# Up projections as one wide and one narrow matmul per slice, 1/rms squared on the down results, and engine reads of interleaved operands reordered, in a two-layer decoder trunk

## The chip, the cores and the metric

The kernel runs on one NeuronCore of a Trainium2 chip. The metric is the device time of one execution in microseconds; smaller is better. Before the change three runs gave 563.83, 562.90 and 562.57 us, a median of 562.9 us. One further execution was profiled; the tables and rows below come from it.

## The reference, cut to what matters

The program is a decoder trunk of two layers over 256 tokens of width 1024. Layer 0 mixes tokens with a gated linear recurrence, layer 1 with sparse attention, and each is followed by a squared-ReLU MLP of width 4096. Every sub-layer sees RMS-normalised input.

```
def _rmsnorm(x, g):
    y = xf * lax.rsqrt(jnp.mean(xf * xf, axis=-1, keepdims=True) + RMS_EPS)
    return (y * g.astype(jnp.float32)).astype(x.dtype)
def _sq_relu_mlp(h, w_up, w_down):
    u = jax.nn.relu(h @ w_up)
    return (u * u) @ w_down
for i in range(DEPTH):
    x = x + (_rglru_mixer if i % 2 == 0 else _nsa_mixer)(_rmsnorm(x, norm_mix[i]), ...)
    x = x + _sq_relu_mlp(_rmsnorm(x, norm_ffn[i]), mlp_w_up[i], mlp_w_down[i])
```

The factor 1/rms is one number per token, so it commutes with every matmul over the width; and relu(r z)² = r² relu(z)² for a positive r.

## The kernel before, in words

Activations are kept transposed, 128 channels on the partitions and 256 tokens along the row. The residual is `xt`, eight such chunks. All large products are made in a 32-bit format with a short mantissa (`F32R`), so each operand is held as a high and a low part, and a product is the sum high·high + high·low + low·high.

**Weights.** 181 pieces, mostly 128 x 1024 (512 KB), stream in through one DMA queue into five `raw` buffers. ScalarE casts a piece to `whi`; VectorE subtracts to give `wlo`. Seven buffers each hold them, and splitting runs up to six pieces ahead of use (`LOOK`). One piece feeds one output chunk of an up projection (eight slices of 128 in the inner dimension) or a quarter of a down chunk.

**Products.** `mm3` makes three matmuls of 256 columns per slice into the same half of a PSUM bank: `whi` with the high activations, `whi` with the low ones, `wlo` with the high ones. `mm2` makes two: `whi` with high and low side by side (512 columns, the two halves of a bank), then `wlo` with high (256 columns, added to the second half); the two halves have to be added afterwards. Before the change `mm2` is used in the down projections alone (15 of their 16 output chunks); the up projections, the mixers' projections and the last down chunk of layer 1 use `mm3`.

**Walked operands.** TensorE reads an activation row in the order 0, 128, 1, 129, ... (`walk`), so a token's place in PSUM is interleaved: PSUM place 2a+i holds token 128i+a. An engine that goes from PSUM to a plain row, or from a plain row to something that TensorE has to find in that order, must undo it. Before, the engines read PSUM in its own order (`pairs`) and stepped through the SBUF operands with `walk`, 512 bytes up, then back, at every element. This is so where projections leave PSUM (L679, L740, L796, L911, L923, L960) and where high and low parts are made of activations (L802, L803, `xbh` and `xbl` in `product`, `oh` and `ol` in `pv`).

**Order of the work.** Two sections (recurrence of layer 0; attention of layer 1) are planned: each step is added to a `Plan` with an engine, a cost, keys it reads and writes and a wished-for time; a list scheduler with a seeded shuffle, then six rounds of backward and forward placing, yields one order per engine, which the engines then follow strictly. So a step taken out anywhere can reorder other steps. The MLPs (`mlp`) are written out in order. Each section ends with `lead_in`, the first three up chunks of the MLP behind it, together with the sums of squares for 1/rms (`stats_wide`: two matmuls against ones, a square root on ScalarE with its table loaded beforehand, a reciprocal of 128 x 256 on VectorE).

**An up chunk** ends with `up_post`: VectorE takes relu(z)·(1/rms) out of PSUM into `t` (L796), ScalarE squares it twice, once plain (`u`, L801) and once rounded and walked into the high part (L802), VectorE subtracts for the low part (L803). `tick` puts the next weight split between. **A down chunk** (32 slices) ends with two adds of a PSUM half into `xt` (L538), then the epilogue, which makes the next layer's operands or the output. The last chunk of layer 1 is seeded: two matmuls with the identity (L824, L825) put `xt` into PSUM first, and `finish` takes the final norm from there: squares (L1303), sums by matmuls against ones (L1305 for the other seven chunks, L1306 for this one), square root, reciprocal, and spreading matmuls (L1312, L1314).

## Time and profile before

| Quantity | Value |
|---|---|
| Median of three runs | 562.9 us |
| Profiled execution: time, span | 563.95 us, 561.8 us |
| Mean granted TensorE clock | 0.996 of full |
| TensorE matmul, busy | 550.5 us, 98% of the span, 4422 instructions |
| VectorE, busy | 436.3 us, 78% |
| ScalarE, busy | 358.0 us, 64% |
| DMA, mean | 184 GB/s over the span |

The stages, by the places of their instructions in the trace: recurrence from 0 to about 95 us, up projection of layer 0 to about 175, its down projection to about 259, attention to about 383, up projection of layer 1 to about 467, its down projection to 553.6, then the final norm and the output.

How to read it: the time of the execution includes some 2.15 us outside the span of its instructions. Matmuls overlap one another, so the busy sum of TensorE says little; the distance from one matmul's start to the next one's says what it costs. A row of the timeline has its start, its length, the engine, the line of the code, the operation, output and inputs, shapes, and in brackets the idle time ahead of it with what ended that.

### The profile page before, as it was taken

Reading aid. Unit: us, or ns where it says so; the run is one execution under the profiler, and the core shown is the slowest. Engines: PE = TensorE matmul, PEld = TensorE weight load, DVE = VectorE, ACT = ScalarE, POOL = GpSimd, SP = SyncE. Lnnn points to the kernel's source line nnn. Section 1 sums busy time; section 2 is a strip of 40 time slices with the busy share of each in tenths; the row PEclk is TensorE's granted clock in tenths of the full one; section 3 lists DMA queues with packets and bytes.
Section 4 is the critical chain, followed back from the end, with each engine's and each line's share of the span. In section 5 each row is a group of like instructions: output and inputs, shape, how many; then the busy total and the mean of one; then the engine's idle time right before and its main releaser. Section 6 shows DMA issues by size and latency. Waiting matters only on the chain.

```text
span 561.8 us, 11456 instructions
## 1 busy us (share of the span) xinstructions
PE 550.5 (98%) x4422; PEld 528.5 (94%) x4422; DVE 436.3 (78%) x888; ACT 358.0 (64%) x670; POOL 40.1 (7%) x55
## 2 busy tenths in 40 slices
PE   9999899999999999999999999999999999999995
PEld 9989899999999999999899998989999999999995
DVE  6899999887788476476849999989988887465532
ACT  7699587777666354354646999977776765353321
POOL 1010000000000131131000000000000000142220
PEclk9999999999999999999999999999999999999998
DMA  8927266576566646655675432263586667556402
GB/s 313 409 90 226 83 225 215 174 234 200 191 194 222 223 161 214 225 167 198 219 229 177 143 104 58 76 211 99 200 239 200 191 213 234 182 187 218 158 1 76
DMA packets 33222, 103.61 MB, mean 184 GB/s; under 512 B 3856, under 2 KB 8080, under 8 KB 33168
## 3 DMA queue, kind: packets, MB, share of 16 engines
q1 hardware_dynamic: 32624, 102.42, 55.5%
q8 instruction: 35, 0.57, 0.4%
q10 hardware_dynamic: 544, 0.46, 0.2%
q14 instruction: 19, 0.16, 0.1%
HBM read 99.23 MB, written 1.05 MB: 179 GB/s over the span
## 4 chain that ended last, share of the span: by engine, by line
PE 73%; DVE 18%; DMA 5%; ACT 2%; issue 1%; SPq 0%; POOL 0%; DVEq 0%; ACTq 0%; POOLq 0%
PE bank L333 19%; PE bank L329 13%; PE bank L330 13%; PE bank L328 13%; PE bank L335 9%; DVE wlo L338 4%; DMA raw<-in_dram 3%; DVE pt L1140 2%; DMA gw<-in_dram 2%; DVE pt L1168 2%; DVE xb L683 1%; DMA pt<-tt 1%; DVE tt L911 1%; DVE t L735 1%; PE bank L1036 1%
## 5 line engine op out<-in xcount | busy, mean ns | idle before, releaser
L328 PE MATMUL bank<-hhl,whi 128*128 128x256 f32 x768 | 212.0, 276 | 0.4 <-DVE tt L960 0.4
L330 PE MATMUL bank<-hhl,wlo 128*128 128x256 f32 x768 | 211.5, 275 | 0.0
L329 PE MATMUL bank<-hhl,whi 128*128 128x256 f32 x768 | 211.5, 275 | 0.0
L333 PE MATMUL bank<-uhl,whi 128*128 128x512 f32 x480 | 157.3, 382 | 0.0
L328 PEld LDWEIGHTS bank<-hhl,whi 128*128 128x128 f32 x768 | 147.7, 192 | 0.6 <-DVE tt L960 0.4
L330 PEld LDWEIGHTS bank<-hhl,wlo 128*128 128x128 f32 x768 | 147.7, 192 | 0.0
L329 PEld LDWEIGHTS bank<-hhl,whi 128*128 128x128 f32 x768 | 147.7, 192 | 0.0
L287 DVE TENSOR_TENSOR wlo<-raw,whi 128x1024 fp32r<-128x1024 f32 x115 | 142.8, 1262 | 1.9 <-ACT whi L278 1.9
L335 PE MATMUL bank<-uhl,wlo 128*128 128x256 f32 x480 | 130.8, 273 | 0.0
L278 ACT CAST whi<-raw 128x1024 fp32r<-128x1024 f32 x116 | 120.0, 1056 | 14.1 <-ACT whi L278 11.0
L333 PEld LDWEIGHTS bank<-uhl,whi 128*128 128x128 f32 x480 | 90.7, 189 | 12.6
L335 PEld LDWEIGHTS bank<-uhl,wlo 128*128 128x128 f32 x480 | 92.2, 192 | 0.0
L338 DVE TENSOR_TENSOR wlo<-raw,whi 128x1024 fp32r<-128x1024 f32 (+2 forms) x72 | 77.1, 1091 | 1.9 <-ACT whi L341 1.8
L341 ACT CAST whi<-raw 128x1024 fp32r<-128x1024 f32 (+2 forms) x64 | 61.1, 969 | 15.4 <-DMA raw<-in_dram 7.3
L538 DVE TENSOR_TENSOR xt<-xt,bank 128x256 f32<-128x256 f32 x54 | 22.3, 419 | 62.2 <-PE bank L335 60.2
L796 DVE SCALAR_TENSOR_TENSOR t<-bank,rstd 128x256 f32<-128x256 f32 x64 | 39.5, 622 | 22.7 <-PE bank L330 22.6
L801 ACT ACTIVATE u<-t 128x256 f32<-128x256 f32 x64 | 26.7, 417 | 45.1 <-DVE t L796 44.9
L803 DVE TENSOR_TENSOR uhl<-u,uhl 128x256 fp32r<-128x256 f32 x64 | 40.8, 638 | 2.7 <-ACT uhl L802 2.6
L802 ACT ACTIVATE uhl<-t 128x256 fp32r<-128x256 f32 x64 | 42.5, 664 | 0.0
L514 ACT ACTIVATE hhl<-xt,vec 128x256 fp32r<-128x256 f32 x8 | 4.1, 508 | 41.4 <-DVE xt L538 41.4
L1143 ACT ACTIVATE pt<-pt,mx 128x128 f32<-128x128 f32 (+1 forms) x64 | 28.6, 449 | 2.0 <-DVE mx L1140 2.0
L1295 ACT ACTIVATE xg<-xt,vec 128x256 f32<-128x256 f32 x7 | 3.6, 508 | 37.7 <-DVE xt L538 37.7
(206 smaller groups left out, 764.1 us busy)
## 6 DMA issues: line engine op xcount, KB each, us to landing
raw<-in_dram SPq DMA_DIRECT2D x171, 512.0 KB, 4.3
raw<-in_dram SPq DMA_DIRECT2D x4, 560.0 KB, 4.5
gw<-in_dram SPq DMA_DIRECT2D x4, 512.0 KB, 9.2
raw<-in_dram SPq DMA_DIRECT2D x6, 256.0 KB, 4.9
y<-in_dram SPq DMA_DIRECT2D x2, 512.0 KB, 7.5
pT<-in_dram SPq DMA_DIRECT2D x2, 512.0 KB, 6.9
xt<-in_dram SPq DMA_DIRECT2D x3, 256.0 KB, 4.9
kl<-tl SPq DMA_DIRECT2D x8, 64.0 KB, 3.8
```

What stands on the lines that cost most here:

```text
L278: (act.copy if eng is None else eng.tensor_copy)(hi_t[i % NSPL][:, :n], raw_of(i)[:, :n])
L287: (eng or dve).tensor_tensor(lo[:, :n], raw_of(i)[:, :n], hi[:, :n].bitcast(F32), op=OP.subtract)
L328: pe.matmul(ps, wh, xh, start=start, stop=False)
L329: pe.matmul(ps, wh, xl, start=False, stop=False)
L330: pe.matmul(ps, wl, xh, start=False, stop=stop)
L333: pe.matmul(ps.rearrange("p (h a i) -> p h a i", h=2, i=2), wh, xhl.rearrange("p (h i a) -> p h a i", h=2, i=2), start=start, stop=False)
L335: pe.matmul(pairs(ps[:, S:]), wl, xh, start=False, stop=stop)
L338: return lambda e: e.tensor_tensor(o, a, h.bitcast(F32), op=OP.subtract)
L341: return lambda e: (e.copy if e is act else e.tensor_copy)(o, a)
L796: dve.scalar_tensor_tensor(walk(t), pairs(z), 0.0, walk(rs), op0=OP.max, op1=OP.mult)
L802: act.activation(uh[m], pairs(t), AF.Square)
L803: later(lambda: dve.tensor_tensor(ul[m], pairs(u), uh[m].bitcast(F32), op=OP.subtract))
```

## The change

Four things are done.

1. **Up projections by `mm2`.** All 64 up chunks (three of each layer in `lead_in`, which gets `wide=True`, the others in `mlp`) use the whole bank: 512 columns, then 256. `up_post` has one step more: ScalarE copies the second half out of PSUM (`s`), and VectorE adds the first half to it, clamped below at zero, in one custom instruction (`TENSOR_ADD_SAT`).
2. **1/rms squared on the down results.** `up_post` no longer multiplies by 1/rms. `stats_var` leaves mean + eps in `acc` and its reciprocal, the square of 1/rms, in `rs`; there is no square root. A down chunk ends with `down_post`: a copy on ScalarE, then add, multiply by `rs`, add to `xt` on VectorE. In both layers now the last down chunk is made by `mm3` and seeded, with `xt` times (mean + eps), and is then multiplied by `rs` as a whole. In layer 1 `finish` works on the unscaled sum: `before_last`, ahead of the last quarter of that chunk, makes the sums of the other chunks and brings `rs` into columns, and the square root's scale and bias hold them. The table of the square root is loaded at up chunk 20 of each layer instead of in the planned sections.
3. **Places.** Wherever an engine stepped through a walked SBUF operand element by element, it now takes PSUM (or the plain row) at every second place (`evens`: first 0, 2, 4, ..., then 1, 3, 5, ...), and the other operands in two plain halves (`parts`). The stored layout and what TensorE reads stay the same.
4. `ahead` no longer makes the planner wait for `rs`.

```diff
+    def evens(x):
+        return x.rearrange("p (a i) -> p i a", i=2)
+    def parts(x):
+        return x.rearrange("p (i a) -> p i a", i=2)
...
+        def stats_var(self, t):
...
+            self.add("dve", 0.4, lambda e: e.tensor_scalar(acc, st(), 1.0 / D, EPS, op0=OP.mult, op1=OP.add), r=b6,
+                     w=["acc"], t=t + 6)
+            self.add("dve", 1.75, lambda e: e.reciprocal(rs, acc), r=["acc"], w=["rs"], t=t + 6)
...
-            zs = [self.proj("up%d" % layer, m, (0, 1, 2)[m], t + 2.65 * m, 0.66)[0] for m in range(3)]
+            zs = [self.proj("up%d" % layer, m, (0, 1, 2)[m], t + 2.65 * m, 0.66, wide=True)[0] for m in range(3)]
...
-            self.stats_wide(t + 1)
+            self.stats_var(t + 1)
...
-            add("dve", 0.34, lambda e: e.tensor_tensor(walk(x[:, 3:]), pairs(z()), walk(rs), op=OP.mult), r=[zk, "rs"], w=[xk], t=t)
+            add("dve", 0.34, lambda e: e.tensor_tensor(parts(x[:, 3:]), evens(z()), parts(rs), op=OP.mult), r=[zk, "rs"], w=[xk], t=t)
...
-        table(AF.Sqrt, tb + 24)
...
-            def up_post(m, z):
+            def up_post(m, zf):
+                s = tmp.tile([P, S], F32, name="s", tag="s")
+                act.copy(parts(s), evens(zf[:, S:]))
                 t = tmp.tile([P, S], F32, name="t", tag="t")
-                dve.scalar_tensor_tensor(walk(t), pairs(z), 0.0, walk(rs), op0=OP.max, op1=OP.mult)
+                dve._custom_dve(TENSOR_ADD_SAT, out=parts(t), in0=evens(zf[:, :S]), in1=parts(s), s0=BIG, s1=0.0)
...
-                act.activation(uh[m], pairs(t), AF.Square)
-                later(lambda: dve.tensor_tensor(ul[m], pairs(u), uh[m].bitcast(F32), op=OP.subtract))
+                act.activation(uhp[m], evens(t), AF.Square)
+                later(lambda: dve.tensor_tensor(ulp[m], evens(u), uhp[m].bitcast(F32), op=OP.subtract))
+            def down_post(m, zf):
+                s = tmp.tile([P, S], F32, name="s", tag="s")
+                act.copy(s, zf[:, S:])
+                t = tmp.tile([P, S], F32, name="t", tag="t")
+                dve.tensor_tensor(t, zf[:, :S], s, op=OP.add)
+                dve.tensor_tensor(t, t, rs, op=OP.mult)
+                dve.tensor_tensor(xt[:, m], xt[:, m], t, op=OP.add)
...
-                        mm3(z, wh[:, w], wl[:, w], hhw[:, k], hlw[:, k], k == 0, k == KC - 1)
+                        mm2(z, wh[:, w], wl[:, w], hw(k), k == 0, k == KC - 1)
...
-                seeded = last is not None and m == 7
+                seeded = m == 7
...
+                    if seeded and early and j == 3:
+                        early()
...
-                        residual(z, m)
-                        residual(zb, m)
+                        down_post(m, zf)
...
-            add([("act", 0.1 + 0.24 * n, 0.0), ("dve", 0.07 + 0.27 * n, 0.2)], lambda e: copy(ohw[:, oj], ow())(e), r=bk, w=ok,
+            add([("act", 0.1 + 0.24 * n, 0.0), ("dve", 0.07 + 0.27 * n, 0.2)], lambda e: copy(ohp[:, oj], ow())(e), r=bk, w=ok,
...
-        table(AF.Sqrt, te)
```

Three places in the order show what moves. First TensorE at the head of layer 0's MLP, where the third up chunk (bank2) is under way and the sums of squares come (`acch` and `accl` against `onesr`). Before:

```order
L328 MATMUL bank2_1211<-hhl_106,whi5_88 128x256
L329 MATMUL bank2_1211<-hhl_106,whi5_88 128x256
L330 MATMUL bank2_1211<-hhl_106,wlo5_95 128x256
L441 MATMUL bank6_1261<-acch_113,onesr_115 128x256
L442 MATMUL bank6_1261<-accl_114,onesr_115 128x256
L328 MATMUL bank3_1324<-hhl_106,whi6_89 128x256
L329 MATMUL bank3_1324<-hhl_106,whi6_89 128x256
```

Now, at the same place:

```order
L341 MATMUL bank2_1198<-hhl_106,whi5_88 128x512
L342 MATMUL bank2_1198<-hhl_106,wlo5_95 128x256
L466 MATMUL bank6_1230<-acch_113,onesr_115 128x256
L467 MATMUL bank6_1230<-accl_114,onesr_115 128x256
L341 MATMUL bank2_1198<-hhl_106,whi5_88 128x512
L342 MATMUL bank2_1198<-hhl_106,wlo5_95 128x256
```

Each slice has two rows in place of three, and the sums now come two slices ahead of the end of the third chunk, not behind it.

Second, VectorE at the end of the attention section. `ol` is the low part of the last attention output, which TensorE needs to go on; `pT` is a copy that the last attention matmuls need; the `wlo` rows are weight splits for pieces that follow, and `raw1_79` is the raw buffer whose refilling the split of `wlo1_91` sets free. Before:

```order
L1091 TENSOR_TENSOR sq1_112<-sq0_111,cm1_3018 128x128
L338 TENSOR_TENSOR wlo1_91<-raw1_79,whi1_84 128x1024
L341 COPY pT_3002<-bank6_4557 128x384
L338 TENSOR_TENSOR wlo2_92<-raw2_80,whi2_85 128x1024
L538 TENSOR_TENSOR xt_100<-xt_100,bank0_4528 128x256
L338 TENSOR_TENSOR wlo3_93<-raw3_81,whi3_86 128x1024
L338 TENSOR_TENSOR wlo4_94<-raw4_82,whi4_87 128x1024
L338 TENSOR_TENSOR wlo5_95<-raw0_78,whi5_88 128x1024
L338 TENSOR_TENSOR ol_3001<-bank7_4581,oh_3000 128x2x128x2
L338 TENSOR_TENSOR wlo6_96<-raw1_79,whi6_89 128x1024
```

Now:

```order
L1139 TENSOR_TENSOR sq1_112<-sq0_111,cm1_2897 128x128
L345 TENSOR_TENSOR wlo2_92<-raw2_80,whi2_85 128x1024
L564 TENSOR_TENSOR xt_100<-xt_100,bank0_4409 128x256
L348 COPY pT_2881<-bank6_4446 128x384
L345 TENSOR_TENSOR wlo3_93<-raw3_81,whi3_86 128x1024
L345 TENSOR_TENSOR wlo4_94<-raw4_82,whi4_87 128x1024
L345 TENSOR_TENSOR wlo5_95<-raw0_78,whi5_88 128x1024
L345 TENSOR_TENSOR wlo6_96<-raw1_79,whi6_89 128x1024
L345 TENSOR_TENSOR ol_2880<-bank7_4464,oh_2879 128x512
```

The split of `wlo1_91` has gone to an earlier place, the copy to `pT` stands behind a split and an add, and the split of `wlo6_96`, which stood behind `ol`, is now ahead of it.

Third, TensorE in the last quarter of the program's last chunk and in the final norm. `sqh0` and `sqh1` are the squares of the last chunk for the two halves of the tokens, `acc` the sums over the others, `rc0` and `rc1` the final factors. Before:

```order
L330 MATMUL bank3_6467<-uhl_4896,wlo4_94 128x256
L1305 MATMUL bank6_4848<-ones_104,acc_107 128x1
L1306 MATMUL bank6_4848<-ones_104,sqh0_4854 128x1
L1305 MATMUL bank7_4849<-ones_104,acc_107 128x1
L1306 MATMUL bank7_4849<-ones_104,sqh1_4855 128x1
L1312 MATMUL bank6_4848<-cst_101,rc0_4852 128x128
L1312 MATMUL bank7_4849<-cst_101,rc1_4853 128x128
```

Now, between the third quarter and the last one:

```order
L338 MATMUL bank3_6188<-uhl_4746,wlo3_93 128x256
L1352 MATMUL bank6_4702<-ones_104,acc_107 128x1 x2
L1354 MATMUL bank7_4703<-cst_101,rstd_108 128x1 x2
L336 MATMUL bank3_6188<-uhl_4747,whi4_87 128x256
L337 MATMUL bank3_6188<-uhl_4747,whi4_87 128x256
```

And now behind the last quarter:

```order
L338 MATMUL bank3_6188<-uhl_4754,wlo4_94 128x256
L1362 MATMUL bank6_4702<-ones_104,sqh0_4710 128x1
L1362 MATMUL bank7_4703<-ones_104,sqh1_4711 128x1
L1368 MATMUL bank6_4702<-cst_101,rc0_4708 128x128
L1368 MATMUL bank7_4703<-cst_101,rc1_4709 128x128
L1370 MATMUL bank0_4704<-cst_101,rc0_4708 128x128
```

The two matmuls over `acc` went ahead of the last quarter, together with two transposes of `rs` that are new, and only those over the last chunk's squares are left behind it.

More of the change, by code (lines that the diff above doesn't have):

```diff
@@ L11 @@
 from concourse._compat import with_exitstack
+from concourse.dve_ops import TENSOR_ADD_SAT
 F32 = mybir.dt.float32
@@ L27 @@
 EPS = 1e-6
+BIG = 3.4028235e38
 NVCOL = 560
@@ L330, in mm3, with mm2 @@
         pe.matmul(ps, wl, xh, start=False, stop=stop)
-    def mm2(ps, wh, wl, xhl, xh, start, stop):
-        pe.matmul(ps.rearrange("p (h a i) -> p h a i", h=2, i=2), wh, xhl.rearrange("p (h i a) -> p h a i", h=2, i=2),
-                  start=start, stop=False)
-        pe.matmul(pairs(ps[:, S:]), wl, xh, start=False, stop=stop)
+    def mm2(ps, wh, wl, xhl, start, stop):
+        pe.matmul(ps.rearrange("p (h a i) -> p h a i", h=2, i=2), wh, xhl, start=start, stop=False)
+        pe.matmul(pairs(ps[:, S:]), wl, xhl[:, 0], start=False, stop=stop)
     def diff(o, a, h):
@@ L446, in stats_wide, with sums @@
             self.add("dve", 1.75, lambda e: e.reciprocal(rs, rs), w=["rs"], t=t)
+        def stats_var(self, t):
+            b6 = [("ps", 6)]
+            st = self.bank(("stats", t), 6, zcols)
+            self.add("act", 0.31, copy(ah, acc), r=["acc"], w=["ah"], t=t)
+            self.add("dve", 0.34, diff(al, acc, ah), r=["acc", "ah"], w=["al"], t=t)
+            def sums(e):
+                e.matmul(st(), onesr, ah, start=True, stop=False)
+                e.matmul(st(), onesr, al, start=False, stop=True)
+            self.add("pe", 0.23, sums, r=["ah", "al"], w=b6, t=t)
+            self.add("dve", 0.4, lambda e: e.tensor_scalar(acc, st(), 1.0 / D, EPS, op0=OP.mult, op1=OP.add), r=b6,
+                     w=["acc"], t=t + 6)
+            self.add("dve", 1.75, lambda e: e.reciprocal(rs, acc), r=["acc"], w=["rs"], t=t + 6)
         def norm(self, m, gcol, t):
@@ L782, in trunk_kernel, with mlp @@
         sec.emit(SEEDS[0])
-    def mlp(layer, epilogue, first, last=None):
+    def mlp(layer, epilogue, first, last=None, early=None):
         with ExitStack() as ph:
@@ L816, in mlp @@
                 zf = next(zrot)
-                z, zb = zf[:, :S], zf[:, S:]
-                seeded = last is not None and m == 7
-                if last and m == 6:
+                z = zf[:, :S]
+                seeded = m == 7
+                if m == 6:
                     act.copy(ir, ident)
-                    act.copy(xh, xt[:, 7])
-                    diff(xl, xt[:, 7], xh)(dve)
+                    t = tmp.tile([P, S], F32, name="t", tag="t")
+                    dve.tensor_tensor(t, xt[:, 7], var, op=OP.mult)
+                    act.copy(xh, t)
+                    diff(xl, t, xh)(dve)
                 if seeded:
@@ L832, in mlp @@
                         else:
-                            mm2(zf, wh[:, w], wl[:, w], uhl[i], uh[i], i == 0, i == NF - 1)
-                    if j == 3 and seeded:
+                            mm2(zf, wh[:, w], wl[:, w], uw[i], i == 0, i == NF - 1)
+                    if j == 3 and seeded and last:
                         last(z)
+                    elif j == 3 and seeded:
+                        dve.tensor_tensor(xt[:, m], z, rs, op=OP.mult)
+                        epilogue(m)
                     elif j == 3:
-                        residual(z, m)
-                        residual(zb, m)
+                        down_post(m, zf)
                         epilogue(m)
@@ L910, in qchunk @@
             ak, bk = ("sa", c % NQ), ("sb", c % NQ)
-            add("dve", 0.4, lambda e: e.scalar_tensor_tensor(walk(x), pairs(z()), cst[:, C_QS + c:C_QS + c + 1], walk(rs),
+            add("dve", 0.4, lambda e: e.scalar_tensor_tensor(parts(x), evens(z()), cst[:, C_QS + c:C_QS + c + 1], parts(rs),
                                                              op0=OP.mult, op1=OP.mult), r=[zk, "rs"], w=[xk], t=t)
@@ L1297, in trunk_kernel, with before_last @@
     sts, dup = [bank(6), bank(7)], [bank(0), bank(1)]
+    bia, scl = (fin.tile([P, 2], F32, name=a) for a in ("bia", "scl"))
     rcs, sqh = ([fin.tile([P, n], F32, name="%s%d" % (a, i)) for i in range(2)] for a, n in (("rc", 1), ("sqh", P)))
     tok = [slice(0, P), slice(P, S)]
+    def before_last():
+        st, sr = sts[0][:, :2], sts[1][:, :2]
+        for i in range(2):
+            pe.matmul(st[:, i:i + 1], acc[:, tok[i]], ones, start=i == 0, stop=i == 1)
+        for i in range(2):
+            pe.transpose(sr[:, i:i + 1], rs[:1, tok[i]], ident[:1, :1])
+        dve.tensor_scalar(bia, st, 1.0 / D, EPS, op0=OP.mult, op1=OP.add)
+        act.activation(scl, sr, AF.Square, scale=D ** -0.5)
     def finish(z):
@@ L1304, in finish @@
         for i in range(2):
-            pe.matmul(sts[i][:, :1], acc[:, tok[i]], ones, start=True, stop=False)
-            pe.matmul(sts[i][:, :1], sqh[i], ones, start=False, stop=True)
-        dve.tensor_scalar(xg[:, 7], z, vec[:, V_GL + 7:V_GL + 8], None, op0=OP.mult)
+            pe.matmul(sts[i][:, 2:3], sqh[i], ones, start=True, stop=True)
+        dve.scalar_tensor_tensor(xg[:, 7], z, vec[:, V_GL + 7:V_GL + 8], rs, op0=OP.mult, op1=OP.mult)
         for i in range(2):
-            act.activation(rcs[i], sts[i][:, :1], AF.Sqrt, bias=epst, scale=1.0 / D)
+            act.activation(rcs[i], sts[i][:, 2:3], AF.Sqrt, bias=bia[:, i:i + 1], scale=scl[:, i:i + 1])
         for i in range(2):
```

41 lines of the change are left out of this document (26 added, 15 removed).

## The prediction, made before the changed kernel was run

> **What bounds the kernel now.** I read the page first, then the windows by stage, then the distances between matmul starts, then the waits of TensorE one by one. The page's first part:
>
> ```profile
> PE 550.5 (98%) x4422; PEld 528.5 (94%) x4422; DVE 436.3 (78%) x888; ACT 358.0 (64%) x670; POOL 40.1 (7%) x55
> ```
>
> TensorE is covered nearly throughout, so only two things shorten the program: less matmul time, or fewer of its few waits. The windows (length, then busy time and count of PE, PEld, DVE, ACT, POOL; clock; DMA) are late recurrence, up projection, layer boundary and attention:
>
> ```profile
> 25.00:72.00 47.00, 45.49 (x342) 42.90 (x340) 46.87 (x86) 39.34 (x68) 2.37 (x7) 1.00 0.47 157
> 120.00:140.00 20.00, 20.00 (x182) 20.00 (x181) 16.29 (x23) 14.16 (x24) 0.00 (x0) 1.00 0.63 203
> 265.00:285.00 20.00, 18.94 (x186) 18.31 (x186) 15.22 (x21) 10.89 (x18) 0.00 (x0) 1.00 0.76 245
> 285.00:376.00 91.00, 89.70 (x840) 84.33 (x836) 83.69 (x372) 76.92 (x223) 0.58 (x4) 1.00 0.42 128
> ```
>
> The up projection is TensorE alone: busy 20.00 of 20 us, VectorE with 3.7 and ScalarE with 5.8 us to spare. In the recurrence VectorE is busy 46.87 of 47 us and TensorE is not: there VectorE sets the pace. In attention both are close. Clock 1.00 everywhere, so it stays out.
>
> What a slice costs is read from starts, since matmuls overlap. In the timeline of the up projection, two rows that both begin a slice, 33 slices apart (99 matmuls), and in the chain that ended last, two rows that begin a slice of the down projection, 20 slices apart:
>
> ```profile
> 119.76 0.28 PE L328 MATMUL bank<-hhl,whi 128*128 128x256 f32 x1
> 130.81 0.28 PE L328 MATMUL bank<-hhl,whi 128*128 128x256 f32 x1
> 179.79 0.22 PE bank L333
> 186.34 0.22 PE bank L333
> ```
>
> Three matmuls of 256 columns: 11.05/33 = 0.3348 us. One of 512 and one of 256: 6.55/20 = 0.3275 us. The columns are equally many; the second form is 7.3 ns shorter per slice.
>
> Then the instructions that the change touches, in the groups by shape (busy us, mean ns):
>
> ```profile
> L796 DVE SCALAR_TENSOR_TENSOR t<-bank,rstd 128x256 f32<-128x256 f32 x64 | 39.5, 622 | 22.7 <-PE bank L330 22.6
> L538 DVE TENSOR_TENSOR xt<-xt,bank 128x256 f32<-128x256 f32 x54 | 22.3, 419 | 62.2 <-PE bank L335 60.2 <-PE bank L330 1.4
> L801 ACT ACTIVATE u<-t 128x256 f32<-128x256 f32 x64 | 26.7, 417 | 45.1 <-DVE t L796 44.9
> L802 ACT ACTIVATE uhl<-t 128x256 fp32r<-128x256 f32 x64 | 42.5, 664 | 0.0
> L278 ACT CAST whi<-raw 128x1024 fp32r<-128x1024 f32 x116 | 120.0, 1056 | 14.1 <-ACT whi L278 11.0 <-PE bank L333 3.1
> L740 DVE TENSOR_TENSOR y<-bank,rstd 128x256 f32<-128x256 f32 x8 | 4.9, 618 | 0.0
> L338 DVE TENSOR_TENSOR xbl<-y,xbh 128x512 fp32r<-128x512 f32 x4 | 4.4, 1099 | 0.1
> L747 DVE TENSOR_TENSOR y<-y,t 128x512 f32<-128x512 f32 x4 | 2.7, 674 | 0.0
> ```
>
> Walking costs: L796 and L740 take 0.62 us where plain L538, also out of PSUM, takes 0.42; `xbl` takes 1.10 where plain L747 of the same size takes 0.67; ScalarE's L802 0.66 against 0.42. That is 0.2 us per 256 columns.
>
> **The change, part by part.** The sum is made against the profiled execution, 563.95 us (span 561.8 and 2.15 around it), which is 1.05 us above the median of 562.9; the same difference is then taken from the median.
>
> *Up projections.* 64 chunks of 8 slices, 512 slices, each 7.3 ns shorter: 3.8 us less, all on TensorE and so on the path, if the end of a chunk keeps up. It has 8 x 0.3275 = 2.62 us. ScalarE then does the copy `s`, two squares and a weight cast: 0.42 + 0.42 + 0.66 + 1.06 = 2.56 us even if walking gains nothing (by plain lengths 2.32); VectorE loses its multiply and keeps an instruction of L796's place; its 16.29 of 20 us become no more. Both fit, and weight splits run up to six pieces, 15 us, ahead, so a small shortfall would not reach TensorE within 32 chunks. Bounds: 0 and 3.8; I take 3.8, as the down projection already runs this form from equal operands.
>
> That `up_post` no longer waits for 1/rms removes nothing: TensorE did not wait there. The square root's table load moves from the planned sections into chunk 20, and the reciprocal is only needed at the first down chunk; both lie under matmuls. Cost nothing; if ScalarE had no room at chunk 20, the load would come out of the 15 us of splits ahead.
>
> *Last down chunk of layer 0.* It goes from `mm2` to `mm3` and gets two seeds. The seeds' price, and two prices for the end, from the timeline of layer 1's seeded chunk and of the tail, and from the view of line 990, a transpose of `rstd` like the new ones:
>
> ```profile
> 542.44 0.29 PE L824 MATMUL bank<-xh,ir 128*128 128x256 f32 x1
> 542.68 0.27 PE L328 MATMUL bank<-uhl,whi 128*128 128x256 f32 x1
> 554.17 0.36 PE L1305 MATMUL bank<-ones,acc 128*128 128x1 f32 x2
> 554.40 0.36 PE L1306 MATMUL bank<-ones,sqh 128*128 128x1 f32 x2
> L990 PE MATMUL bank<-cst,rstd x2: 196/207/218, 270.6 to 270.7; 1*128 1x1 f32 x2
> ```
>
> Seeds 0.24 us, 32 x 7.3 ns = 0.23: +0.47. The other down chunks get a copy and one VectorE step more per 10.5 us of matmuls: nothing.
>
> *Tail.* Two sums over `acc` (0.23 each by the starts above) and two transposes (some 0.1 to 0.2 each) move under the last quarter as TensorE time: +0.7. Behind the last matmul the second sum over `acc` no longer stands between the two sums of squares: -0.23. Net +0.45, bounds 0.2 and 0.9.
>
> *Places, in the recurrence.* TensorE's waits there, in the timeline (idle time in brackets; a matmul of 256 normally starts 0.11 us after the one before):
>
> ```profile
> 65.56 0.28 PE L330 MATMUL bank<-xbh,wlo 128*128 128x256 f32 x1
> 66.31 0.38 PE L328 MATMUL bank<-xbh,whi 128*128 128x256 f32 x1 [0.48 <-ACT xbh L341]
> 67.72 0.38 PE L329 MATMUL bank<-xbl,whi 128*128 128x256 f32 x1 [1.03 <-DVE xbl L338]
> 71.95 0.28 PE L328 MATMUL bank<-xbh,whi 128*128 128x256 f32 x1
> 72.44 0.38 PE L329 MATMUL bank<-xbl,whi 128*128 128x256 f32 x1 [0.21 <-DVE xbl L338]
> ```
>
> Lost: 0.64 + 1.30 + 0.38 = 2.3 us, all behind VectorE and the walked cast `xbh`. The trace has no read at every second place, so its cost is bounded: at best the plain length (L538, L747), a saving of 0.2 us per 256 columns; at the other end, bounds below. At best, by 67.7 us VectorE has saved 8 x 0.2 (`xp`) + 5 x 0.2 (`y`) + 0.43 (`xbl`) = 3.0 us, more than the 1.94 us of the first two waits, and the last goes likewise: -2.3. I take the best end, because two of its places lie 8 bytes apart where today each element is a jump of 512 bytes.
>
> [...]
>
> *Places, at the layer boundary.* TensorE waits for the reciprocal and for VectorE's `tt`:
>
> ```profile
> 270.05 0.28 PE L330 MATMUL bank<-hhl,wlo 128*128 128x256 f32 x1
> 270.61 0.28 PE L990 MATMUL bank<-cst,rstd 1*128 1x1 f32 x2 [0.28 <-DVE rstd L446]
> 276.96 0.29 PE L1038 MATMUL bank<-whi,hhl 128*128 128x304 f32 x1
> 277.68 0.38 PE L1036 MATMUL bank<-whi,hhl 128*128 128x256 f32 x1 [0.43 <-DVE tt L960]
> ```
>
> 0.45 and 0.59 us. The last chunk now ends with one VectorE step where two adds of 0.42 stood, and each `tt` may be 0.2 shorter; but the way to the reciprocal leads through weight splits that wait for TensorE. I take -0.6, bounds 0 and -1.0.
>
> *Attention.* The last wait, with VectorE and ScalarE:
>
> ```profile
> 374.24 0.28 PE L330 MATMUL bank<-oh,wlo 128*128 128x256 f32 x1
> 374.59 0.38 PE L328 MATMUL bank<-oh,whi 128*128 128x256 f32 x1
> 375.71 0.38 PE L329 MATMUL bank<-ol,whi 128*128 128x256 f32 x1 [0.74 <-DVE ol L338]
> 372.53 1.05 ACT L341 CAST whi<-raw 128x1024 fp32r<-128x1024 f32 x1 [2.43 <-DMA raw<-in_dram]
> 366.89 1.22 DVE L338 TENSOR_TENSOR wlo<-raw,whi 128x1024 fp32r<-128x1024 f32 x1
> 374.57 1.09 DVE L338 TENSOR_TENSOR ol<-bank,oh 128x512 fp32r<-128x512 f32 x1 [1.09 <-ACT oh L341]
> ```
>
> 0.24 + 1.01 us: a weight piece lands late, its cast holds `oh` in ScalarE's queue, `oh` holds `ol`. The new order splits `wlo1_91` (the row at 366.89, which frees that piece's buffer) earlier, so the piece comes earlier; against that, `ol` now queues behind one split more. From 366.89 VectorE has a split, an add, a copy and four splits (five times near 1.15 us by the row of 366.89 less its overlap, 0.4, and some 0.5 by estimate), near 6.6 us, so `ol` starts near 373.5 and ends near 374.2 (plain) or 374.6 (as now); TensorE asks at 374.35. I take -1.0 there and -0.2 for the rest, whose order is shuffled too; bounds -2.3 and +1.3 (the end's wait twice as long).
>
> *Sum.* -3.8 + 0.47 + 0.45 - 2.3 - 0.6 - 1.2 = -7.0. The profiled execution would take 556.95 us, the median 555.9.
>
> **The rivals.**
>
> *No gain from places.* A read at every second place costs what the hop does, 0.62 us. Then the recurrence keeps its waits, the boundary gives 0.2 and attention 0.6 (the buffer freed earlier): -3.8 + 0.92 - 0.8 = -3.7, 559.2 us. For it: PSUM reads are in most of these instructions, and no row shows one with gaps. [...]
>
> *Dearer places, the slower side.* If the extra is doubled, 0.4 instead of 0.2 us per 256 columns, VectorE, full already, is 3.0 us later at 67.7 and later again for the next pairs: +4.0 there; +0.5 at the boundary; in attention nine evacuations and four `ol`, 3.5 us on an engine busy 83.7 of 91, half of it on the path with the end: +2. Sum -2.9 + 6.5 = +3.6, 566.5 us. It decides from about 0.1 us beyond today's 0.62, where 6.5 x 0.1/0.2 outweighs 2.9.
>
> *The shuffle loses.* The moved split in front of `ol` and other moved steps give attention +0.4 instead of -1.2: 557.5 us. For it: the planner's costs and rules know nothing of the late piece.
>
> *The up projection does not speed up,* because a chunk's end with its extra hand-over from ScalarE to VectorE holds banks: 559.7 us. Against it: six banks rotate.
>
> **How the numbers follow.** Forecast 0.52, no gain from places 0.25, shuffle 0.10, no up gain 0.05, dearer places 0.08. A measurement here tells about 0.2%, 1.1 us, from no change. The first four are all over 2 us faster; with 0.04 kept for mixtures near zero: faster 0.88, same 0.04, slower 0.08. Low end: every wait gone and the small costs at their least, -9.0, with a little beyond it: 553.5. High end: no gain from places with a small loss in attention: 560.0. Outside lie the dearer places and about a tenth for the unforeseen.
>
> **What would show it.** Right: in the up projection slices 0.3275 us apart; L740's successor near 0.42 us and `xbl` near 0.67; no wait over 0.3 us between 64 and 73 us; the wait in front of the last `ol` under 0.5 us. Wrong: evacuations at 0.6 us or more, VectorE still full to 72 us, or up slices still 0.335 apart.

## The result, and the profile after

The changed kernel took 554.36 us (median of four runs, 554.28 to 554.80) against 563.16 for the kernel before on the same chip: a ratio of 0.9845, with a 95% interval of 0.9828 to 0.9862. That is 8.8 us less, 1.6%. The forecast was 555.9 us. The profiled execution took 554.28 us, with a span of 552.4; before it was 563.95 and 561.8.

Page and windows of the changed kernel, in the columns known from before (length, then PE, PEld, DVE, ACT, POOL; clock; DMA):

```profile
PE 544.3 (99%) x3946; PEld 512.1 (93%) x3946; DVE 424.0 (77%) x907; ACT 372.6 (67%) x751; POOL 39.9 (7%) x55
```

```profile
25.00:72.00 47.00, 46.91 (x358) 45.03 (x358) 46.61 (x88) 39.74 (x68) 2.17 (x7) 1.00 0.50 169
120.00:140.00 20.00, 20.00 (x125) 18.41 (x124) 14.65 (x23) 15.31 (x32) 0.00 (x0) 1.00 0.69 212
262.00:282.00 20.00, 19.83 (x205) 19.36 (x204) 13.46 (x23) 10.60 (x21) 0.00 (x0) 1.00 0.81 286
282.00:370.00 88.00, 88.00 (x829) 84.00 (x828) 81.51 (x372) 74.91 (x220) 0.58 (x4) 1.00 0.40 126
```

TensorE is now covered in all four stretches. In the up projection it has two matmuls per slice in place of three (125 in 20 us for 182), and ScalarE rose from 14.16 to 15.31 us. VectorE is as full in the recurrence as it was, 46.61 of 47 us.

The groups by shape that answer to those of before (busy us, mean ns of one):

```profile
L833 ACT ACTIVATE uhl<-t 128x256 fp32r<-128x256 f32 x64 | 32.3, 504 | 0.0
L834 DVE TENSOR_TENSOR uhl<-u,uhl 128x256 fp32r<-128x256 f32 x64 | 30.4, 475 | 0.0
L827 DVE CUSTOM_DVE_ANT_0 t<-bank,s 128x256 f32<-128x256 f32 x64 | 27.1, 423 | 34.1 <-ACT s L825 33.9
L825 ACT COPY s<-bank 128x256 f32<-128x256 f32 x64 | 23.5, 368 | 20.2 <-PE bank L342 20.1
L766 DVE TENSOR_TENSOR y<-bank,rstd 128x256 f32<-128x256 f32 x8 | 3.3, 415 | 0.0
L345 DVE TENSOR_TENSOR xbl<-y,xbh 128x512 fp32r<-128x512 f32 x4 | 2.9, 730 | 0.0
```

Out of PSUM the price of walking is gone entirely: `y` takes 415 ns where it took 618. Out of SBUF some is left: `xbl` 730 ns, where walking took 1099 and the plain instruction 674. In the timeline of the recurrence, TensorE's only wait for `xbl` that is left to speak of, 0.36 us from start to start where 0.11 is normal:

```profile
65.34 0.28 PE L336 MATMUL bank<-xbh,whi 128*128 128x256 f32 x1
65.70 0.38 PE L337 MATMUL bank<-xbl,whi 128*128 128x256 f32 x1
```

Two rows that begin a slice of the up projection, 33 slices apart, then the last `ol` and the matmul that needs it (0.12 us from the row ahead of it, so no wait; it was 1.12):

```profile
119.62 0.38 PE L341 MATMUL bank<-hhl,whi 128*128 128x512 f32 x1
130.43 0.38 PE L341 MATMUL bank<-hhl,whi 128*128 128x512 f32 x1
...
366.70 0.68 DVE L345 TENSOR_TENSOR ol<-bank,oh 128x512 fp32r<-128x512 f32 x1
367.32 0.28 PE L336 MATMUL bank<-oh,whi 128*128 128x256 f32 x1
367.44 0.38 PE L337 MATMUL bank<-ol,whi 128*128 128x256 f32 x1
```

The slices are (130.43 - 119.62)/33 = 0.3276 us apart. The tail, squares to spreading matmuls, in the timeline, and the early sums in the view of their line (durations in ns, first and last start):

```profile
544.14 0.45 ACT L1360 ACTIVATE sqh<-bank 128x128 f32<-128x128 f32 x2 [2.70 <-PE bank L338]
544.47 0.61 PE L1362 MATMUL bank<-ones,sqh 128*128 128x1 f32 x4 [0.37 <-ACT sqh L1360]
544.89 0.59 ACT L1365 ACTIVATE rc<-bank,bia,scl 128x1 f32<-128x1 f32 x2 [0.31 <-PE bank L1362]
545.27 0.41 DVE L1367 RECIPROCAL rc<-rc 128x1 f32<-128x1 f32 x2 [0.17 <-ACT rc L1365]
545.49 0.73 PE L1368 MATMUL bank<-cst,rc 128*128 128x128 f32 x4 [0.42 <-DVE rc L1367]
```

```profile
L1352 PE MATMUL bank<-ones,acc x4: 169/250/250, 540.5 to 540.8; 128*128 128x1 f32 x4
```

The stages, cut at the starts of TensorE's matmuls in both traces, beside the prediction's terms:

| Stage | before | after | difference | predicted |
|---|---|---|---|---|
| start to the first down matmul (recurrence, up 0) | 175.37 | 170.71 | -4.66 | -2.3 - 1.9 |
| down 0 | 83.73 | 84.21 | +0.48 | +0.47 |
| boundary, to attention's first transposes | 23.45 | 22.20 | -1.25 | -0.6 |
| attention, to the last output matmul | 100.41 | 97.56 | -2.85 | -1.2 |
| up 1 | 86.12 | 84.19 | -1.93 | -1.9 |
| down 1 | 84.21 | 84.95 | +0.74 | +0.7 |
| tail | 8.47 | 8.55 | +0.08 | -0.23 |

The differences add up to -9.4 us, which is the difference of the two spans; the medians differ by 8.8, since the profiled execution of the kernel before took 0.8 us more than its median. In the first row 0.33 us lie ahead of the first matmul of the recurrence's output projection (65.00 us before, 64.67 now). TensorE's order changed at the end of that projection as well: before, two slices of the up projection (0.67 us) stand ahead of its last matmul, now none does.

### The profile page after: what moved, and what is told of

Same layout as the page of the kernel before. It is cut to its first block, busy times and chain, and to the rows that moved or that the text cites. A ratio compares the mean times of both kernels' runs of the same rounds, so it can differ in the third digit from the quotient of the medians.

```text
span 552.4 us, 10583 instructions
## 1 busy us (share of the span) xinstructions
PE 544.3 (99%) x3946; PEld 512.1 (93%) x3946; DVE 424.0 (77%) x907; ACT 372.6 (67%) x751; POOL 39.9 (7%) x55
## 4 chain that ended last, share of the span: by engine, by line
PE 89%; DVE 5%; ACT 4%; issue 0%; POOL 0%; DVEq 0%; ACTq 0%; POOLq 0%
PE bank L341 38%; PE bank L342 19%; PE bank L337 7%; PE bank L336 7%; PE bank L338 7%; PE bank L1250 3%; PE bank L1231 2%; PE bank L1177 1%; PE bank L1178 1%; DVE wlo L345 1%; PE bank L609 1%; DVE t L761 1%; PE bank L1084 1%; ACT t L738 1%; PE bank L1085 1%; PE bank L1086 1%
## 5 line engine op out<-in xcount | busy, mean ns | idle before, releaser
L341 PE MATMUL bank<-hhl,whi 128*128 128x512 f32 x512 | 167.9, 382 | 0.0
L341 PE MATMUL bank<-uhl,whi 128*128 128x512 f32 x448 | 146.8, 382 | 0.0
L342 PE MATMUL bank<-uhl,wlo 128*128 128x256 f32 x448 | 122.1, 273 | 0.0
L341 PEld LDWEIGHTS bank<-hhl,whi 128*128 128x128 f32 x512 | 96.8, 189 | 13.3
L341 PEld LDWEIGHTS bank<-uhl,whi 128*128 128x128 f32 x448 | 84.7, 189 | 11.8
L342 PEld LDWEIGHTS bank<-uhl,wlo 128*128 128x128 f32 x448 | 86.0, 192 | 0.0
L336 PE MATMUL bank<-hhl,whi 128*128 128x256 f32 x256 | 71.2, 278 | 0.2 <-DVE tt L1008 0.2
L337 PE MATMUL bank<-hhl,whi 128*128 128x256 f32 x256 | 70.8, 277 | 0.0
L827 DVE CUSTOM_DVE_ANT_0 t<-bank,s 128x256 f32<-128x256 f32 x64 | 27.1, 423 | 34.1 <-ACT s L825 33.9
L336 PEld LDWEIGHTS bank<-hhl,whi 128*128 128x128 f32 x256 | 49.4, 193 | 0.3 <-PE bank L1038 0.2
L337 PEld LDWEIGHTS bank<-hhl,whi 128*128 128x128 f32 x256 | 49.4, 193 | 0.2
L838 ACT COPY s<-bank 128x256 f32<-128x256 f32 x14 | 5.2, 372 | 58.5 <-PE bank L342 58.5
L840 DVE TENSOR_TENSOR t<-bank,s 128x256 f32<-128x256 f32 x14 | 5.9, 425 | 50.0 <-ACT s L838 50.0
L825 ACT COPY s<-bank 128x256 f32<-128x256 f32 x64 | 23.5, 368 | 20.2 <-PE bank L342 20.1
```

The source lines that it names most:

```text
L336: pe.matmul(ps, wh, xh, start=start, stop=False)
L337: pe.matmul(ps, wh, xl, start=False, stop=False)
L341: pe.matmul(ps.rearrange("p (h a i) -> p h a i", h=2, i=2), wh, xhl, start=start, stop=False)
L342: pe.matmul(pairs(ps[:, S:]), wl, xhl[:, 0], start=False, stop=stop)
L825: act.copy(parts(s), evens(zf[:, S:]))
L827: dve._custom_dve(TENSOR_ADD_SAT, out=parts(t), in0=evens(zf[:, :S]), in1=parts(s), s0=BIG, s1=0.0)
```

## The experiments

The theory: three separate gains, the shorter matmuls of the up projections, shorter engine steps in the recurrence, and shorter steps in boundary and attention. The rivals: that the new order of the plan made what attention gained, that the new end of layer 0's last down chunk made it, or that the chunk's end in the MLPs has a price that the rest hides. "The stage" below is boundary and attention together. All edit the changed kernel, but for one that gives the kernel before the places alone. The changed kernel's first 65 us, up to the first matmul of the output projection, differ by up to 1 us between profiled executions of the same instructions, so an edit is judged first in its own stage. Those stages vary less, but they do vary: where nothing in it was edited, the output projection took 21.81 to 22.32 us, attention 97.56 to 97.92. Each stage figure below is that of one profiled execution.

**The changed kernel again.** Unedited, beside the later runs.

> The changed kernel itself, beside the run below that differs by half a microsecond from it. Theory: 554.4 us within 0.4, with a first stage, up to the first matmul of the output projection, that varies by up to 1 us from one profiled execution to the next (63.7 to 64.8 us so far with the same code there). Rival: the half microseconds by which the undone versions differ are of the size of its own spread, so it could be read anywhere from 553.7 to 555.2.

It took 553.82 us (553.74 to 554.45), ratio 0.9847 [0.9833, 0.9860]. The two medians, 554.36 and 553.82, are 0.5 us apart; differences below are against 554.1, and less than half a microsecond says nothing by itself. By stages this execution agrees with the first within 0.05 us everywhere behind the first 65 us.

**Recurrence walked again.**

```
-    tensor_tensor(parts(y_t[m]), evens(z()), parts(rs), ...)      # xp likewise
+    tensor_tensor(walk(y_t[m]), pairs(z()), walk(rs), ...)
-    y, h, l_, x = (... (y_b, xbh_b, xbl_b, t_b)), read at every second place
+    y, h, l_, x = (... (y_b, xbhw, xblw, t_b))
```

> The changed kernel with the places of the recurrence undone: xp, y, xbh and xbl step through walked SBUF operands element by element again; everything else and the order of every engine stay. Theory (the recurrence gained because VectorE's and ScalarE's steps there became shorter): the 2.8 us by which recurrence and first up projection shortened beyond the matmuls' own 1.9 come back, so about 557.2 us, with y near 0.62 us, xbl near 1.10 and TensorE waits of together 2 to 2.8 us between 64 and 73 us. Rival (the up chunks in front of the MLP are what ended the waits: fewer matmuls, sums of squares earlier, a shorter plan): at most half comes back, 554.4 to 555.7 us, and the waits stay small.

556.55 us, ratio 0.9885 [0.9870, 0.9900], so about 2.4 us slower. The waits of TensorE in its timeline, and the groups:

```profile
65.76 0.38 PE L336 MATMUL bank<-xbh,whi 128*128 128x256 f32 x1 [0.47 <-ACT xbh L348]
67.19 0.38 PE L337 MATMUL bank<-xbl,whi 128*128 128x256 f32 x1 [1.05 <-DVE xbl L345]
71.90 0.38 PE L337 MATMUL bank<-xbl,whi 128*128 128x256 f32 x1 [0.20 <-DVE xbl L345]
```

```profile
L345 DVE TENSOR_TENSOR xbl<-y,xbh 128x512 fp32r<-128x512 f32 x4 | 4.4, 1095 | 0.1
```

All three waits of the kernel before are back, each within 0.02 us of its old length, and the output projection takes 24.28 us in place of 21.86. The theory holds: the new up chunks in front of the MLP did nothing to these waits. Of the 2.8 us that it expected, 0.33 lie ahead of the output projection, where executions differ anyway. The cure is not always complete: in five of the eleven executions whose recurrence is as changed, TensorE still waits for the first `xbl`, 0.35 to 0.56 us, the longest in the run with the old order in attention (below). So the places are worth 1.96 to 2.47 us here.

```profile
65.28 0.38 PE L337 MATMUL bank<-xbl,whi 128*128 128x256 f32 x1 [0.56 <-DVE xbl L345]
```

**Boundary and attention walked again** (L959, L971, L1008, `oh`, `ol`; the engines keep the new order).

```
-    tensor_tensor(parts(x), evens(z()), parts(rs), op=OP.mult)
+    tensor_tensor(walk(x), pairs(z()), walk(rs), op=OP.mult)
-    copy(ohp[:, oj], ow()) ... diff(olp[:, oj], ow(), ohp[:, oj])
+    copy(ohw[:, oj], ow()) ... diff(olw[:, oj], ow(), ohw[:, oj])
```

> The changed kernel with the places of the layer boundary and of attention undone: the products that leave the q, k and c projections, and the high and low parts of the attention outputs, step through walked SBUF operands again; the order of every engine stays. Theory (the 4.1 us of the stage from the boundary to the last attention output are mostly places): 3 to 4 us come back, 557.4 to 558.4 us, with waits of 0.3 us and more at several of the projections and 0.5 or more in front of the last ol. Rival (the new order of the plan made most of it, above all the earlier split that frees the late weight piece's buffer): 1.5 us or less come back, 554.4 to 555.9 us, and the wait for the last ol stays under 0.5 us.

556.41 us, ratio 0.9880 [0.9865, 0.9895]: 2.3 us slower, and 2.22 in the stage (121.99). Neither theory's number came: more than the rival's 1.5, less than 3. Two of the waits that came back, the second being the last `ol`:

```profile
324.96 0.37 PE L1177 MATMUL bank<-kh,sb 128*128 128x288 f32 x1 [0.26 <-DVE cm L1195]
369.75 0.38 PE L337 MATMUL bank<-ol,whi 128*128 128x256 f32 x1 [0.67 <-DVE ol L345]
```

The first stands behind another `ol`: VectorE does that one from 323.68 for 1.12 us (0.68 in the changed kernel), and the step that TensorE waits for is queued behind it.

**The old order in attention.** One line back in the planned section, with which VectorE and ScalarE follow the kernel before's order word for word through attention.

```
+        table(AF.Sqrt, te)
```

> The changed kernel with one line back, the load of the square root's table as a step of the attention section's plan. With it VectorE and ScalarE follow the kernel before's order word for word from the first projection to the last attention output; all else is as changed. Theory (undoing the places of boundary and attention gave back 2.2 of the stage's 4.1 us; the other 1.9 are the new order): 1.2 to 1.9 us slower than the changed kernel, 555.6 to 556.3, with the wait for the last ol back near 1 us. Rival (with shorter steps the order no longer matters; the 1.9 us come from the boundary and the freed minutes of the reciprocal): within 0.4 us of the changed kernel, 554.0 to 554.8 us.

("Freed minutes" means the time by which the reciprocal comes earlier.) 554.94 us, ratio 0.9854 [0.9836, 0.9871]: 0.8 us slower, between the two expectations; 0.83 in the stage. The late weight piece is back ahead of `oh`, and the last `ol` late (0.69 us from the start ahead of it, where 0.11 is normal). The table's load itself, 1.28 us on ScalarE, comes behind the last `oh` and is not what this `ol` waits for:

```profile
367.86 0.38 PE L337 MATMUL bank<-ol,whi 128*128 128x256 f32 x1 [0.35 <-DVE ol L345]
```

**Both undone.** Walked operands in boundary and attention and the old order.

> The changed kernel with both undone in boundary and attention: walked operands there, and the line that brings back the old order of VectorE and ScalarE. Theory (places 2.1 and order 1.9, which add up): about 4 us slower than the changed kernel, 558.4 us, the stage from the boundary to the last attention output near 123.8 us. Rival (the last down chunk's new end and the early reciprocal shorten the boundary by themselves): 0.5 to 1.9 us of the stage stay, 556.5 to 557.9 us, and then the waits missing are those before 279 us.

557.63 us, ratio 0.9900 [0.9881, 0.9918]: 3.5 us slower. The stage takes 122.55 us, not the 123.86 of the kernel before: the rival has it, 1.31 us stay. They lie where it said, before attention's first transposes (22.31 us against 23.45), while attention itself is back, 100.24 against 100.41. With the two runs above this makes a square for attention: neither 100.24, the new order alone 99.68, places alone 98.40, both 97.56. Places are worth 1.84 to 2.12 us there, the order 0.56 to 0.84; beside the 0.36 us by which unedited executions differ, the order's share is the less certain one.

**Places alone, in the kernel before.** Its up projections, 1/rms and plan stay.

```
-    dve.scalar_tensor_tensor(walk(t), pairs(z), 0.0, walk(rs), op0=OP.max, op1=OP.mult)
+    dve.scalar_tensor_tensor(parts(t), evens(z), 0.0, parts(rs), op0=OP.max, op1=OP.mult)
     (and so at every other walked operand)
```

> The kernel before with the places alone: every second place read wherever it walked, nothing else; its up projections, 1/rms and plan stay. Theory (recurrence 2.3, boundary and attention 2.1, chunk ends of the MLPs nothing): 562.9 less 4.4, about 558.5 us. Rival (places make the old order harmless too, so that all 4.1 us of attention come without the new one): about 556.5 us. By the view that a read at every second place costs as much as walking: 562.9.

557.51 us, ratio 0.9901 [0.9884, 0.9918]: 5.4 us faster than before, a microsecond more than the theory and a microsecond less than the rival. Its output projection, with the two up slices in it as before, takes 22.52 us for 24.93 (-2.41), boundary 22.65 for 23.45 (-0.80), attention 98.13 for 100.41 (-2.28). The boundary explains most of the theory's miss: the wait of 0.59 us for `tt` goes when its steps get shorter, and it also goes when the reciprocal comes earlier, so each cure alone gets it (-0.80 here, -1.14 with walked operands and the new chunk end) and both together only -1.25. Undoing one showed little, doing one showed much.

**Layer 0's last down chunk without seeds,** made like the other seven.

```
-                seeded = m == 7
-                if m == 6:
+                seeded = last is not None and m == 7
+                if last and m == 6:
```

> The changed kernel with the last down chunk of layer 0 made like the other seven: two matmuls a slice, no seeds, and behind it copy, add, multiply and add in place of one multiply. Theory (the end of that chunk hides under the projections that start the next layer with other chunks): the 0.47 us of seeds and narrow matmuls are saved, 553.9 us. Rival (the end is on the path of the sums of squares and of the last chunk's operands: about 0.37 + 0.42 + 0.42 us longer, of which the boundary hides little): 0.3 to 0.8 us slower, 554.7 to 555.2 us, with waits at the head of the q, k and c projections.

554.95 us, ratio 0.9853 [0.9833, 0.9873]: 0.85 us slower by the medians. The down stage gets its 0.48 us back (83.73), the boundary grows by 1.31 (23.51), so the rival holds, at the top of its range. In its timeline:

```profile
264.86 1.74 DVE L456 RECIPROCAL rstd<-rstd 128x256 f32<-128x256 f32 x1
266.66 0.28 PE L1038 MATMUL bank<-cst,rstd 1*128 1x1 f32 x2 [1.16 <-DVE rstd L456]
```

The reciprocal starts 10.58 us behind the last down matmul; in the changed kernel it is 9.27, in the kernel before 9.71. Copy, add, multiply and add in place of one multiply are on the path to it, and TensorE waits 1.16 us. So the seeds, which look like a loss of 0.48 us in their own stage, are what lets the reciprocal be early.

**Up chunks' ends walked again.** `s`, `t` and both parts of the square.

> The changed kernel with the places of the up chunks' ends undone: s, t and both parts of the square step through walked operands again. Theory (VectorE's and ScalarE's steps there lie under TensorE's 2.62 us per chunk, with weight splits some 15 us ahead): at most 0.5 us slower, 554.3 to 554.9 us, TensorE without a wait in the up projections. Rival (with two matmuls per slice ScalarE has no room: copy, two squares and a weight cast would take 0.62 + 0.42 + 0.66 + 1.05 = 2.75 us of 2.62 a chunk, so the splits fall behind): 64 x 0.13 = up to 8 us slower less what the pieces ahead take up, so 556 to 562 us, with waits of TensorE for whi or wlo late in an up projection or at the head of the down projection.

554.06 us, ratio 0.9839 [0.9825, 0.9854]: no difference, as the theory had it. A window of its up projection, and the copy out of PSUM with its walked output:

```profile
110.00:170.00 60.00, 60.00 (x368) 55.24 (x367) 54.65 (x76) 58.12 (x103) 0.00 (x0) 1.00 0.70 222
```

```profile
L825 ACT COPY s<-bank 128x256 f32<-128x256 f32 x64 | 42.8, 669 | 3.7 <-PE bank L342 3.7
```

ScalarE is busy 58.12 of 60 us (50.00 with places) and TensorE still never waits. The new places are worth nothing in the 64 chunks where there are most of them.

**Up projections of three matmuls again,** the rest as changed.

```
-    mm2(z, wh[:, w], wl[:, w], hw(k), k == 0, k == KC - 1)
+    mm3(z, wh[:, w], wl[:, w], hhw[:, k], hlw[:, k], k == 0, k == KC - 1)
-    (the copy s and the custom add)
+    dve.tensor_scalar(parts(t), evens(zf), 0.0, None, op0=OP.max)
```

> The changed kernel with the up projections by three matmuls of 256 columns per slice, and a chunk's end that clamps straight out of PSUM on VectorE, without the copy s and the addition; 1/rms stays on the down results, squared, and the places stay. Theory (the wide form alone gives the up projections' gain, 7.3 ns a slice): 3.75 us slower, 558.1 us, slices 0.335 us apart. Rival (the gain of the up stage came from the chunk's end that no longer waits for 1/rms, or from the lead-in of the plan, not from the matmuls): under 1.5 us slower, 554.4 to 555.9 us.

558.05 us, ratio 0.9910 [0.9894, 0.9927]: 3.9 us slower, where 3.75 were expected. Both up stages grow by 1.92 us. The starts of two slices, 33 apart, are 11.06/33 = 0.335 us a slice:

```profile
119.73 0.28 PE L336 MATMUL bank<-hhl,whi 128*128 128x256 f32 x1
130.79 0.28 PE L336 MATMUL bank<-hhl,whi 128*128 128x256 f32 x1
```

**The sums over `acc` back behind the last matmul.**

```
     def finish(z):
         for i in range(2):
             act.activation(sqh[i], z[:, tok[i]], AF.Square)
+        for i in range(2):
+            pe.matmul(st[:, i:i + 1], acc[:, tok[i]], ones, start=i == 0, stop=i == 1)
+        dve.tensor_scalar(bia, st, 1.0 / D, EPS, op0=OP.mult, op1=OP.add)
         ...   (and both are gone from before_last)
```

> The changed kernel with the two sums over acc, and the bias made from them, back behind the last matmul, ahead of the sums over the last chunk's squares; the two transposes stay early. Theory (the sums are 0.46 us of TensorE time in the last quarter, but behind the last matmul TensorE idles 0.37 us for sqh anyway, so they are free there): last down stage 84.5 in place of 84.95 us, tail 8.55 to 8.65, in all 0.35 to 0.46 us faster than the changed kernel. Rival (the bias becomes the last thing that the square root waits for, since it comes 0.2 to 0.3 us behind the second sum): the tail grows by 0.3 us or more and nothing is left, 0.1 faster to 0.1 slower.

553.72 us, ratio 0.9840 [0.9827, 0.9854]: not to be told from the changed kernel by the medians (553.82 beside it). By stages the theory has it, at its low edge: down 84.62 in place of 84.96, tail 8.50 in both.

```profile
543.78 0.50 PE L1360 MATMUL bank<-ones,acc 128*128 128x1 f32 x4
544.31 0.61 PE L1363 MATMUL bank<-ones,sqh 128*128 128x1 f32 x4
544.32 0.16 DVE L1361 TENSOR_SCALAR bia<-bank 128x2 f32<-128x2 f32 x1 [9.91 <-PE bank L1360]
544.73 0.59 ACT L1366 ACTIVATE rc<-bank,bia,scl 128x1 f32<-128x1 f32 x2 [0.30 <-PE bank L1363]
```

The sums fit between the last matmul and the squares, and the bias is done a quarter of a microsecond ahead of the square root.

**What a hop costs.** Two kernels with other steps in the chunk's end (`ev` and `pt` stand in place of `evens` and `parts`), one execution each (554.67 and 553.84 us).

```
+            n = (1, 128)[layer]          # and (4, 16)
+            ev = lambda x: x.rearrange("p (a i) -> p i a", i=n)
+            pt = lambda x: x.rearrange("p (i a) -> p i a", i=n)
```

> The changed kernel with other places in the up chunks' ends, for the lengths of the instructions alone: in layer 0 no reordering at all (step 1), in layer 1 reads at every 128th place (0, 128, 1, 129, ...), written plainly; the tokens come out in another order than the computation needs. Theory (a hop costs on the side where it is made, read or write, PSUM or SBUF): step 1: s near 0.37, t 0.42, the rounded square 0.42, ul 0.42 us; step 128: all like walking, s 0.67, t 0.63, the square 0.67, ul 0.64. Rival (walking cost by its writes alone, PSUM reads at any step are free): step 128 leaves s and t at 0.37 and 0.42. The rounded type costs nothing by itself: if step 1 has the square at 0.50 instead, the 0.09 us at step 2 are the type's and not the places'.

> As before, with reads at every 4th place in layer 0 and every 16th in layer 1; the tokens come out in another order than the computation needs. [...] Rival (PSUM reads are free at any step up to 16, SBUF's small extra of step 2 stays what it is): s 0.37, t 0.42, the square 0.50, ul 0.48 us in both layers.

Mean ns of one instruction of 128x256, reads at every nth place and plain writes, from these two and the changed kernel; in the last column, walked as in the run with the up chunks' ends walked:

| | step 1 | 2 | 4 | 16 | 128 | walked |
|---|---|---|---|---|---|---|
| `s`, ScalarE out of PSUM | 369 | 368 | 369 | 376 | 370 | 669 |
| `t`, VectorE out of PSUM | 424 | 423 | 424 | 423 | 423 | 634 |
| rounded square, ScalarE out of SBUF | 407 | 504 | 849 | 660 | 470 | 673 |
| `ul`, VectorE out of SBUF | 416 | 475 | 805 | 605 | 420 | 639 |

The ends of it in the groups, layer 1 with step 128 and layer 0 with step 4:

```profile
L836 ACT ACTIVATE uhl<-t 128x256 fp32r<-128x256 f32 x32 | 15.0, 470 | 0.0
L828 ACT COPY s<-bank 128x256 f32<-128x256 f32 x32 | 11.8, 370 | 10.9 <-PE bank L342 10.9
```

```profile
L836 ACT ACTIVATE uhl<-t 128x256 fp32r<-128x256 f32 x32 | 27.2, 849 | 0.0
L828 ACT COPY s<-bank 128x256 f32<-128x256 f32 x32 | 11.8, 369 | 1.4 <-PE bank L342 1.4
```

No reading order out of PSUM that was tried costs anything (368 to 376 ns on ScalarE, 423 or 424 on VectorE), so for PSUM the rival is right in both runs. For SBUF the first run's theory (0.67 and 0.64 us at step 128) is wrong, since 470 and 420 ns came, and so is the second run's rival (0.50 and 0.48 us at both steps): 849 and 805 ns at step 4, 660 and 605 at 16. Nor does the price simply grow with the distance: 16 places cost less than 4, and 128 less again. The walked `s` reads PSUM in its own order, so its 0.30 us (669 ns against 369) can only be its hopping writes. The rounded type has no price (407 ns at step 1, where the plain square `u` of the same chunks took 420), so the 0.1 us of step 2 (504 ns) are the places'.

## Why the prediction was right, and where its sizes were off

The gains came from where the prediction said. By the medians it was 8.8 us in place of 7.0, so the forecast of 555.9 us was 1.5 us too long, and the measured time lies nearer the low end of the range. In the stage table the terms are short by 2.4 us: attention by 1.65, boundary by 0.65 and the first row by 0.46, against 0.37 that the tail cost more.

- *Up projections, -3.8.* Right: slices 0.3276 us apart, -3.75 us by undoing, as sized. The chunk's end fits, even walked (58.12 of 60 us).
- *Layer 0's last chunk, +0.47.* Right, +0.48.
- *Recurrence, -2.3.* Right: undoing gives 2.42 us in the output projection (1.96 to 2.47 beside the other executions). The best end that was taken, the plain length, is right for PSUM (`y` took 415 ns, plain L538 419) and nearly right for SBUF (`xbl` took 730, plain L747 674); no row of before showed such a read, so this was a choice between bounds that came out, not a reading. Its reason, the shorter jump, is not borne out: SBUF reads at step 128, a jump of 512 bytes at every element, took 470 and 420 ns where step 2 took 504 and 475. One sign that was to show it right, no wait over 0.3 us between 64 and 73 us, holds in the changed kernel's two profiles and fails in five others with the same recurrence. One sign that was to show it wrong was badly chosen: VectorE is full to 72 us all the same, since it now does 14 weight splits in that window where it did 12. A queue that always has splits waiting says little by being full.
- *Boundary, -0.6.* Too small: -1.25, outside the bound of -1.0. Shorter end and shorter `tt` each suffice for the wait of 0.59 us, which is gone, and the reciprocal starts 0.4 us earlier than before, about the one add that went; its wait gives 0.35 us. A third wait was left out of the prediction's list, that of the first matmul behind the transposes of `rstd`, also for `tt`. It is 0.17 us idle now and was, in the timeline before:

```profile
271.24 0.38 PE L328 MATMUL bank<-hhl,whi 128*128 128x256 f32 x1 [0.35 <-DVE tt L960]
```

- *Attention, -1.2 (-1.0 at its end, -0.2 for the rest).* This is the step whose size failed: -2.85. From the last score matmul on it gave 1.56 us, ahead of that 1.29. The rival of the dearer places counted nine evacuations and four `ol` as work on an engine busy 83.7 of 91 us; the same count was not made for the gain. The waits before the end (0.28 us idle at 330.16 in the trace before, behind an `ol`) were visible and were put under "the rest".
- *Tail, +0.45.* Too small by 0.37: +0.74 and +0.08. The early sums cost as sized, but the -0.23 for the second sum over `acc` did not come. From the start of the squares to the spreading matmuls it was 1.26 us (553.60 to 554.86 in the trace before) and is 1.35. That second sum belonged to the second half of the tokens, while the chain goes through the first; and from the start of `rc` to the reciprocal, 0.29 us became 0.38. The square root `rc` itself takes 347 ns where it took 262. Its scale is now read from a column, as its bias was before; that this is the cause is not shown.
- *The rivals.* "No gain from places" and "dearer places" fall with the lengths of the instructions (no run shows the doubled extra of 0.4 us per 256 columns: at every second place these took 423 ns out of PSUM, and 475 and 504 out of SBUF), "the up projection does not speed up" with its stage. "The shuffle loses" had the wrong sign: the new order is worth 0.56 to 0.84 us, in good part by the mechanism named, the earlier split that lets the late piece come (when it is undone, the last `ol` starts its matmul 0.58 us late).

Out of SBUF the new places shorten the instructions too, if not to the plain length: a read at every second place costs 59 ns more than a plain one on VectorE (475 against 416) and 97 on ScalarE (504 against 407), where the walked instruction costs 223 and 266 more (639 and 673). So "no gain from places" is wrong there as well. Out of PSUM step 2 costs nothing (423 against 424 ns on VectorE, 368 against 369 on ScalarE), and most of the changed instructions that mattered read PSUM.

What stays open: why VectorE's and ScalarE's SBUF reads are dearest at step 4 of the steps tried (805 and 849 ns), whether VectorE's walked writes alone make up its 0.21 us (its walked instructions read a walked operand too), and what makes the first 65 us vary by a microsecond from one execution to the next.

## What to carry to other kernels

When an interleaving has to be undone, read PSUM with the hops and write plainly: every reading order out of PSUM that was tried was free here (368 to 376 ns on ScalarE and 423 or 424 on VectorE, at steps of 1 to 128), while hopping writes cost 0.30 us per 256 columns on ScalarE (669 ns against 369), and VectorE's walked instructions took 0.16 to 0.21 us more than the new ones. Such a gain counts only where the engine is waited for: in 64 chunk ends under matmuls it was worth nothing (554.06 us with them walked, 554.1 without), and in some 50 steps of the mixers and the boundary it brought 5.4 us by itself. When pricing an edit, make for the gain the same count over a full engine that is made for the loss, and expect two cures of one wait to be worth little more than one.

## What the runs showed of the hardware that was not expected

Reads of SBUF at a step of four 32-bit places are twice as long as plain ones (805 against 416 ns on VectorE, 849 against 407 on ScalarE), while a step of 128 places, which only alternates between two runs, costs 4 and 63 ns. Reads of PSUM cost the same at steps of 1, 2, 4, 16 and 128 on both engines (423 to 424 ns on VectorE, 368 to 376 on ScalarE).
